# An encoder layer with two groups of attention heads: the grid heads' matrix work in equal sets with scores six steps ahead, value transposes in projection banks, the last projection ended half by half

## The chip, the core and the metric

One Trainium2 chip, of which one core is used. The core has a matrix engine (TensorE, PE in the rows; its weight loads are PEld), a vector engine (VectorE, DVE), a scalar engine (ScalarE, ACT), a fourth engine (GpSimd, POOL), and a queue engine (SyncE, SP) that issues DMAs. Each engine takes its own instructions in order; semaphores make one wait for another. Matrix products land in PSUM, of which this kernel uses eight banks of 128 partitions x 512 float32. The metric is the device time of one execution in microseconds (us); lower is better.

## What is computed

One layer on `x` of 1024 tokens x 1024 features, in float32: a normalized projection, two token mixers side by side, an output projection, and a gated MLP. Cut to the parts that the change touches:

```python
hn = rmsnorm(x, norm_mix)
qa, ka, va, qb, kb, vb = split(hn @ w_in)       # 1024 x 2304
# group A: 8 heads of 64, 2 key/value heads, |i - j| <= 128, rotary, a sink logit
o_a = window_gqa_sink(rope(qa), rope(ka), va, sink)
# group B: 8 heads of 64; tokens are a grid of 16 rows x 64 columns,
# each attends to a window of 8 x 16 grid positions, with a bias per head and offset
o_b = neighbourhood_attention(qb, kb, vb, rpb)
mix = concat(rmsnorm(o_a, norm_a), rmsnorm(o_b, norm_b))
h = x + mix @ w_out
out = rmsnorm(h + conv_gated_mlp(rmsnorm(h, norm_ffn)), norm_final)
```

In group B, for each head: scores `s = q k^T / 8 + bias` over the neighbourhood, `p = softmax(s)`, `o = p v`.

## The kernel before

**Layout and precision.** Features lie on partitions and tokens along the free dimension: eight tiles of 128 x 1024 hold the activations. A product of two float32 matrices is done as three matmuls of a faster type (fp32r) on operands split in a high and a low part, high x high, high x low and low x high. So every operand passes a split first: ScalarE copies the high part, VectorE subtracts it for the low part. A *projection block* is these three matmuls of 512 columns for one 128-row chunk of the contraction: `block()`, L177 to L179.

**Projections.** `Project(m)`, m = 0 to 17, each makes 128 of the 2304 columns of `w_in` for all tokens, in two halves of 512 tokens with 8 blocks each. m < 6 feeds group A, m >= 6 the grid heads (group B): of each three, one makes the values of a pair of heads (6, 9, 12, 15) and the next two make query and key of one head each. Head h's q and k come from m = 7 + h + h // 2, so head 6's from 16 and head 7's from 17, the last. Each projection takes a PSUM bank of the tag `pj` for each half; when a half is done, VectorE multiplies it with the tokens' inverse norm and reorders it (`evacuate()`, L251 for the grid). The projection's operands are `xg`, the split input.

Then the result is made ready for attention (`post()`):
- `split_qk()` for a grid head: for each half, ScalarE writes the scaled high part `a` (L306), VectorE the low part `b` (L307); then four DMAs of 256 KB on SP's queue stack queries and keys: q[0:64] from a (L309), q[64:128] from b (L310), b[0:64] from a (L311), a[0:64] from b (L312). Tile `a` is called ka and `b` kb. L311 overwrites rows that L310 reads.
- `split_v()` for a pair's values: TensorE transposes four chunks of 128 tokens into one bank (L334), ScalarE copies the high part (L338) and VectorE subtracts (L339), for each of the two heads; then the same for the other four chunks. The first group uses a bank of the tag `pj` and is issued at once; the second is put in the list `later` with a count of 2, so that it comes two blocks further on, in a bank of the tag `pt`, which is that of the probability transposes.

Behind the projections, `OutA(d)`, d = 0 to 7, does the half of the output projection that needs group A only, and adds `x` (L623). Its operands `mg` are the split of `mix[0:4]`, made during projection 17 by `split()` (L189 for the high, L190 for the low part, a whole tile of 128 x 1024 each).

**Attention over the grid.** For each of 8 heads and each block b of 128 tokens (8 columns of the grid):
- *score* (`q_step`): two matmuls of 256 or 384 columns (L389), against ka and then kb, into a bank `s`; VectorE adds the bias and takes the extreme in one pass (L412), ScalarE takes exp (L416); at every second block VectorE takes reciprocals (L418) and GpSimd scales the probabilities (L420);
- *transposes* (`t_step`): two or three transposes of 128 x 128 of the probabilities into a bank `pt` (L526); ScalarE copies the high part ph (L426), VectorE makes the low part pl (L427);
- *value product* (`v_step`): a matmul with ph (L537) and one with pl (L538) of 256 or 384 columns into banks `o`, two per head; at a half's end `leave()` moves it out (L552, L554) into mix[4:8].

The window attention of group A has the same three steps, with its own lines (L452 transposes, L457 and L458 value products, L474 the way out).

**Order.** TensorE's order is written by hand: the program's order of matmuls is the engine's. VectorE, ScalarE and the queues are ordered by a scheduler that has priorities (`high_priority`) and a few fixed orders (`behind`). Each tag of PSUM, `pj`, `pt`, `s` and `o`, has two banks that are taken in turn.

The hand-written order mixes attention steps with projection blocks. The attention is a list of *units* u (16 for group A; then four per grid head, with the transposes steps [0], [1, 2], [3, 4] and [5, 6, 7]). In each unit a list of *events* is made: for each transposes step "t", then "v", and scores "q" put between them at fixed places. A "v" runs the value product of the transposes step *before*. After each event, projection blocks come from a generator `filler`, as many as a running `debt` says; `RATES` gives the blocks per eight window units or per grid head. So the blocks between a transposes step and its value product are what covers the split L426 and L427:

```python
            for i, item in enumerate(mine):
                events.insert(min(EVA[i] if kind == 0 else 2 * i + 1, len(events)), ("q", item))
            wi = u // 8 if u < 16 else 2 + (u - 16) // 4
            per = RATES[wi] / (8 if u < 16 else 4) / len(events)
```

The scores taken in unit u are those up to unit u + 2. A score whose projection is not finished makes `run_q` pull blocks from the filler first. `settle()` runs once per block: it counts down `later`, and starts `post()` of a projection LAG = 3 blocks (for 17: SOON = 1) behind its end.

Some other work is put at fixed blocks of the filler: the squares of mix[0:4] (L200), their sums over features (`add_up()`, L209 transposes and L210 the reduction), `widen()` (L240) and the eight normalizations of mix[0:4] with group A's gain (`normed_a`, L816), all during projections 14 to 16; at heads 6 and 7 the squares of mix[4:7] (`square_b`, L880). `halve_w()` (L170 and the line behind it) splits the weights. At the very start, L707 and neighbours are the first three projections, run chunk by chunk as the input arrives; L146 is a set of matmuls on ones ahead of them. The MLP behind the attention has lines from L960 on.

Of the kernel before, what the change touches and what calls it, by code (L numbers as in the profile page):

```python
# [20 lines left out]
KT = D // 128  # L21
# [12 lines left out]
RATES = [41, 50, 21, 21, 21, 21, 13, 19, 20, 17]  # L34
SPARE = (3, 6)
AHEAD = 4
EVA = (1, 3, 5, 8)
# [19 lines left out]
def hybrid_layer(tc, xT, w_first, w_in, w_out, w_gate, w_up, w_down, small, sink, rpb, consts, rope, out):  # L57
    nc = tc.nc
    with ExitStack() as ctx:
# [126 lines left out]

        def split(src, name, tag):
            hi, lo = big(name + "h", tag, F32R), big(name + "l", tag, F32R)
            nc.scalar.activation(hi, src, AF.Copy)  # L189
            nc.vector.tensor_tensor(lo, src, f32(hi[:, :]), op=ALU.subtract)  # L190
            return hi, lo
# [135 lines left out]
        def split_v(t, halves, then=None):  # L327
# [13 lines left out]
            if then is None:  # L341
                group(0)
                group(1)
            else:
                with tc.high_priority(offset=500):
                    group(0, "pj")
                later.append([2, lambda: (group(1), then())])
# [215 lines left out]
        class Project:  # L563
# [10 lines left out]
            def run(self):  # L574
# [7 lines left out]
                else:  # L582

                    ps = [bank("pj", "pj") for _ in range(2)]
                    for k in range(KT):
                        for h in range(2):
                            block(ps[h], self.w[k], xg[k], h, k == 0, k == KT - 1)
                            yield
                        if k % 2:
                            mg[k // 2] = split(mix[k // 2], "mg", "xg")  # L590
                    with tc.high_priority(offset=500):
                        for h in range(2):
                            evacuate(self.t, ps[h], h, self.grid)

            def post(self):
                post(self.m, self.t)
                if self.m < 6 or self.m % 3:
                    done.add(self.m)

# [263 lines left out]
        def run_q(items):  # L863
            for u, s in items:
                while any(m not in done for m in flat[u][2]):
                    assert next(filler)
                s()
# [19 lines left out]
        for u in range(len(flat)):  # L887
            q, t, need, kind = flat[u]
            if kind == 0 and u < 14:
                mine = q_until(u + 2, 4)  # L890
            else:
                mine = q_until(min(u + 2, len(flat) - 1), 99)
            events = []
            for ts in t:
                events += [("t", ts), ("v", None)]
            for i, item in enumerate(mine):
                events.insert(min(EVA[i] if kind == 0 else 2 * i + 1, len(events)), ("q", item))
            wi = u // 8 if u < 16 else 2 + (u - 16) // 4
            per = RATES[wi] / (8 if u < 16 else 4) / len(events)
            if u in (40, 44):  # L900
                square_b(u)
            for what, e in events:
# [9 lines left out]
                fill(int(debt))  # L912
# [696 lines left out]
```

## Time and profile before

| | before |
|---|---|
| time, median of 3 runs | 1026.67 us (1026.21 to 1027.19) |
| time of the profiled execution | 1027.14 us |
| its span on the core, from the first to the last recorded instruction | 1025.3 us |
| TensorE matmuls, busy | 1011.5 us, 99% |
| TensorE weight loads (beside the matmuls) | 890.5 us, 87% |
| VectorE busy | 836.6 us, 82% |
| ScalarE busy | 562.0 us, 55% |
| GpSimd busy | 108.6 us, 11% |

How to read the profile: times are microseconds from the start of the span; an operation is written out<-in by the names of the program's tiles; "L177" is a line of the kernel. A timeline row has the start, the duration, the engine, the line, the operation with its tiles and shapes, and in brackets how long the engine had stood idle before it and which instruction ended that wait. "x3" at the end is three instructions run together in one row. "SPq" is the issue of a DMA from SP's queue. Matmuls are pipelined and their ends are modelled, so that a row's duration is longer than the time until the next one can start. A row of waits has the waiting engine and operation, what released it, the microseconds in all, how often, and the longest.

The attention over the grid runs from about 170 to 352 us, mixed with projections 6 to 17 and OutA.

### The profile page before, as it was taken

How to read it: one execution, taken by the hardware profiler on the slowest of the kernel's cores; microseconds unless marked ns; L12 is line 12 of the kernel's file. 1: busy time of each engine (PE TensorE's matmuls, PEld its weight loads, DVE VectorE, ACT ScalarE, POOL GpSimd, SP SyncE). 2: the span in 40 equal slices, each digit the busy share in tenths (PEclk: the TensorE clock that was granted, in tenths of full speed). 3: DMA queues.
4: the chain of work that ended last, by engine and by line, in shares of the span. 5: the costliest groups of instructions: out<-in, count | busy, mean ns of one | idle time of the engine just before them, and what ended most of it. 6: DMA issues, size and time to landing. Idle time of an engine off the chain costs nothing.

```text
span 1025.3 us, 14859 instructions
## 1 busy us (share of the span) xinstructions
PE 1011.5 (99%) x5094; PEld 890.5 (87%) x5094; DVE 836.6 (82%) x1566; ACT 562.0 (55%) x1077; POOL 108.6 (11%) x188
## 2 busy tenths in 40 slices
PE   9999999999999999999999999999999999999996
PEld 8888888888888888888888888888888888888886
DVE  7889887768878799999987777786787877996765
ACT  8567776657676544565545444443544645554451
POOL 0233332232342100000000000000000000000002
PEclk9999999999999999999999999999999999999999
DMA  7223022323226257213442332233322888966644
GB/s 292 77 77 95 30 73 62 93 72 84 81 62 185 76 161 267 93 61 105 156 186 100 129 117 96 100 113 113 102 108 98 285 295 297 306 228 236 224 151 165
DMA packets 68220, 144.94 MB, mean 141 GB/s; under 512 B 8240, under 2 KB 18736, under 8 KB 68144
## 3 DMA queue, kind: packets, MB, share of 16 engines
q1 hardware_dynamic: 58064, 118.82, 36.1%
q10 hardware_dynamic: 10080, 25.17, 6.3%
q8 instruction: 40, 0.66, 0.3%
q14 instruction: 36, 0.29, 0.1%
HBM read 103.58 MB, written 28.57 MB: 129 GB/s over the span
## 4 chain that ended last, share of the span: by engine, by line
PE 84%; DVE 10%; ACT 4%; issue 2%; DMA 1%; DVEq 0%; POOL 0%; ACTq 0%; POOLq 0%
PE dn L994 7%; PE dn L992 7%; PE dn L993 6%; PE pj L177 6%; PE pj L178 6%; PE pj L179 6%; PE x L992 6%; PE x L993 6%; PE x L994 6%; PE y L994 3%; PE y L993 3%; PE y L992 3%; PE s L389 3%; PE z L994 2%; PE z L992 2%
## 5 line engine op out<-in xcount | busy, mean ns | idle before, releaser
L992 PE MATMUL x<-hg,whi 128*128 128x512 f32 x352 | 133.6, 380 | 0.9 <-ACT gs L1034 0.9
L993 PE MATMUL x<-hg,whi 128*128 128x512 f32 x352 | 133.4, 379 | 0.0
L994 PE MATMUL x<-hg,wlo 128*128 128x512 f32 x352 | 133.4, 379 | 0.0
L992 PE MATMUL dn<-xd,whi 128*128 128x512 f32 (+1 forms) x330 | 120.8, 366 | 0.0
L993 PE MATMUL dn<-xd,whi 128*128 128x512 f32 (+1 forms) x330 | 120.5, 365 | 0.0
L994 PE MATMUL dn<-xd,wlo 128*128 128x512 f32 (+1 forms) x330 | 120.5, 365 | 0.0
L416 ACT ACTIVATE p<-p,nm 128x385 f32<-128x385 f32 (+3 forms) x128 | 75.1, 588 | 53.9 <-DVE nm L412 50.7
L420 POOL TENSOR_SCALAR p<-p,sm 128x384 f32<-128x384 f32 (+1 forms) x128 | 79.7, 635 | 204.6 <-DVE sm L418 177.8
L966 ACT ACTIVATE whi<-ws 128x512 fp32r<-128x512 f32 (+1 forms) x100 | 60.8, 622 | 72.0 <-DVE ws L1106 16.6
L177 PE MATMUL pj<-xgh,whi 128*128 128x512 f32 x245 | 99.7, 407 | 0.0
L178 PE MATMUL pj<-xgl,whi 128*128 128x512 f32 x245 | 92.9, 379 | 0.0
L179 PE MATMUL pj<-xgh,wlo 128*128 128x512 f32 x245 | 92.9, 379 | 0.0
L966 ACT ACTIVATE whi<-raw 128x512 fp32r<-128x512 f32 (+1 forms) x102 | 61.0, 612 | 44.1 <-PE x L993 20.3
L967 DVE TENSOR_TENSOR wlo<-ws,whi 128x512 fp32r<-128x512 f32 (+1 forms) x100 | 66.8, 682 | 19.9 <-ACT whi L966 19.6
L427 DVE TENSOR_TENSOR pl<-pt,ph 128x384 fp32r<-128x384 f32 (+2 forms) x108 | 63.5, 589 | 20.5 <-ACT ph L426 18.4
L1314 ACT ACTIVATE xd<-xd 128x512 fp32r<-128x512 f32 x77 | 47.7, 628 | 53.3 <-DMA xd<-x 52.6
L1429 POOL TENSOR_TENSOR h<-h,wide 128x256 f32<-128x256 f32 (+1 forms) x6 | 5.4, 915 | 670.9 <-ACT wide L1425 670.9
L992 PEld LDWEIGHTS x<-hg,whi 128*128 128x128 f32 x352 | 66.5, 189 | 10.9 <-ACT gs L1034 1.5
L994 PEld LDWEIGHTS x<-hg,wlo 128*128 128x128 f32 x352 | 66.5, 189 | 9.5
L993 PEld LDWEIGHTS x<-hg,whi 128*128 128x128 f32 x352 | 66.5, 189 | 9.3
L1315 DVE TENSOR_TENSOR xd<-xd 128x512 fp32r<-128x512 f32 x77 | 52.5, 690 | 27.0 <-ACT xd L1314 26.8
L992 PEld LDWEIGHTS dn<-xd,whi 128*128 128x128 f32 x330 | 62.5, 189 | 7.7
(267 smaller groups left out, 2535.4 us busy)
## 6 DMA issues: line engine op xcount, KB each, us to landing
xd<-x SPq DMA_DIRECT2D x77, 256.0 KB, 5.1
raw<-in_w_down_dram SPq DMA_DIRECT2D x72, 256.0 KB, 4.4
raw<-in_w_gate_dram SPq DMA_DIRECT2D x22, 512.0 KB, 3.4
raw<-in_w_up_dram SPq DMA_DIRECT2D x22, 512.0 KB, 3.6
x<-c ACTq DMA_DIRECT2D x22, 512.0 KB, 2.6
raw<-in_w_in_dram SPq DMA_DIRECT2D x30, 256.0 KB, 2.8
raw<-in_w_down_dram SPq DMA_DIRECT2D x36, 192.0 KB, 4.5
x<-t ACTq DMA_DIRECT2D x11, 512.0 KB, 2.6
```

The source lines that it names most:

```text
L177: nc.tensor.matmul(ps, w[0], mv(x[0][:, tsl(h)]), start=first, stop=False)
L178: nc.tensor.matmul(ps, w[0], mv(x[1][:, tsl(h)]), start=False, stop=False)
L179: nc.tensor.matmul(ps, w[1], mv(x[0][:, tsl(h)]), start=False, stop=last)
L416: nc.scalar.activation(p[:, j, 0:e], p[:, j, 0:e], AF.Exp, bias=nm, scale=-1.0, accum_out=sm[:, j:j + 1])
L420: nc.gpsimd.tensor_scalar(p[:, i, 0:m], p[:, i, 0:m], sm[:, i:i + 1], 1.0, op0=ALU.mult, op1=ALU.mult)
L427: mark["rest"] = nc.vector.tensor_tensor(pl[:, 0:n], ps[:, 0:n], f32(ph[:, 0:n]), op=ALU.subtract)
L966: nc.scalar.activation(hi, src, AF.Copy)
L967: nc.vector.tensor_tensor(lo, src, f32(hi[:, :, :]), op=ALU.subtract)
L992: nc.tensor.matmul(ps, w[0], x[0], start=first and i == 0, stop=False, skip_group_check=True)
L993: nc.tensor.matmul(ps, w[0], x[1], start=False, stop=False, skip_group_check=True)
L994: nc.tensor.matmul(ps, w[1], x[0], start=False, stop=last and i == len(ws) - 1, skip_group_check=True)
L1315: nc.vector.tensor_tensor(lo, f32(lo), f32(hi), op=ALU.subtract)
```

## The change

The same matmuls, splits and transfers are done in another order and in part in other banks; the last projection's operands are split in other pieces.

- *Equal sets.* In the grid, each transposes step now opens a set of its own: the transposes, one score, the value product of the step before. Each set gets one eighth of the head's projection blocks, spread evenly over its events. Before, a unit's blocks were spread over its events, so a unit with three transposes steps had as many blocks as one with a single step.
- *Scores six steps ahead.* One score is taken per set (three in the first), so that the score of block b + 6 goes with the transposes of chunk b. `GRID_AHEAD = 6`. The last window units take their scores in as before, without a limit of four.
- *Rates.* `RATES` changes by one block in heads 2, 3, 6 and 7. Blocks that `run_q` pulls are now taken off the debt.
- *Second half of the value transposes.* It comes 8 blocks later in place of 2, in a bank of the tag `pj`, at high priority.
- *Last projection.* For the first six chunks the halves alternate as before; then half 0 gets its last two chunks, and half 1 its last two. Each half is evacuated as soon as its last block is issued. The splits of mix[0:4] are done by halves (`split_part`: 128 x 512), eight in place of four of each kind; `split()` is gone.

```diff
@@ -31,9 +31,10 @@
 
 LAG, LATE, SOON = 3, 13, 1
 FILL0, FILL1 = 22, 14
-RATES = [41, 50, 21, 21, 21, 21, 13, 19, 20, 17]
+RATES = [41, 50, 21, 21, 22, 22, 13, 19, 19, 16]
 SPARE = (3, 6)
 AHEAD = 4
+GRID_AHEAD = 6
 EVA = (1, 3, 5, 8)
 WARM = 8
 
@@ -183,12 +184,6 @@
             for i, (w, x) in enumerate(zip(ws, xs, strict=True)):
                 block(ps, w, x, h, i == 0, i == len(ws) - 1)
                 yield
-
-        def split(src, name, tag):
-            hi, lo = big(name + "h", tag, F32R), big(name + "l", tag, F32R)
-            nc.scalar.activation(hi, src, AF.Copy)
-            nc.vector.tensor_tensor(lo, src, f32(hi[:, :]), op=ALU.subtract)
-            return hi, lo
 
         def squares(tiles, engine):
             acc = None
@@ -344,7 +339,12 @@
             else:
                 with tc.high_priority(offset=500):
                     group(0, "pj")
-                later.append([2, lambda: (group(1), then())])
+                def second():
+                    with tc.high_priority(offset=500):
+                        group(1, "pj")
+                    then()
+
+                later.append([8, second])
             return [x[:, :].rearrange("p (c w) -> p c w", w=128) for x in v]
 
         qa, ka, va, qb, kb, vb = {}, {}, {}, {}, {}, {}
@@ -582,20 +582,33 @@
                 else:
 
                     ps = [bank("pj", "pj") for _ in range(2)]
-                    for k in range(KT):
-                        for h in range(2):
-                            block(ps[h], self.w[k], xg[k], h, k == 0, k == KT - 1)
-                            yield
-                        if k % 2:
-                            mg[k // 2] = split(mix[k // 2], "mg", "xg")
-                    with tc.high_priority(offset=500):
-                        for h in range(2):
-                            evacuate(self.t, ps[h], h, self.grid)
+                    order = [(k, h) for k in range(KT - 2) for h in range(2)] + [(k, h) for h in range(2) for k in (KT - 2, KT - 1)]
+                    parts = []
+                    for k, h in order:
+                        block(ps[h], self.w[k], xg[k], h, k == 0, k == KT - 1)
+                        if k == KT - 1:
+                            with tc.high_priority(offset=500):
+                                evacuate(self.t, ps[h], h, self.grid)
+                        yield
+                        if parts:
+                            split_part(*parts.pop(0))
+                        if h and k % 2:
+                            i = k // 2
+                            mg[i] = big("mgh", "xg", F32R), big("mgl", "xg", F32R)
+                            split_part(i, 0)
+                            parts.append((i, 1))
+                    for part in parts:
+                        split_part(*part)
 
             def post(self):
                 post(self.m, self.t)
                 if self.m < 6 or self.m % 3:
                     done.add(self.m)
+
+        def split_part(i, h):
+            src, (hi, lo) = mix[i][:, tsl(h)], (t[:, tsl(h)] for t in mg[i])
+            nc.scalar.activation(hi, src, AF.Copy)
+            nc.vector.tensor_tensor(lo, src, f32(hi), op=ALU.subtract)
 
         class OutA:
             def __init__(self, d):
@@ -861,9 +874,11 @@
             return res
 
         def run_q(items):
+            nonlocal debt
             for u, s in items:
                 while any(m not in done for m in flat[u][2]):
                     assert next(filler)
+                    debt -= 1
                 s()
 
         sums = {}
@@ -886,20 +901,23 @@
         fill(FILL1 - 12)
         for u in range(len(flat)):
             q, t, need, kind = flat[u]
-            if kind == 0 and u < 14:
-                mine = q_until(u + 2, 4)
+            events = []
+            if kind == 0:
+                mine = q_until(u + 2, 4 if u < 14 else 99)
+                for ts in t:
+                    events += [("t", ts), ("v", None)]
+                for i, item in enumerate(mine):
+                    events.insert(min(EVA[i], len(events)), ("q", item))
+                rate = [RATES[u // 8] / 8 / len(events)] * len(events)
             else:
-                mine = q_until(min(u + 2, len(flat) - 1), 99)
-            events = []
-            for ts in t:
-                events += [("t", ts), ("v", None)]
-            for i, item in enumerate(mine):
-                events.insert(min(EVA[i] if kind == 0 else 2 * i + 1, len(events)), ("q", item))
-            wi = u // 8 if u < 16 else 2 + (u - 16) // 4
-            per = RATES[wi] / (8 if u < 16 else 4) / len(events)
+                rate = []
+                for ts in t:
+                    mine = q_until(len(flat) - 1, 1 if events or u > 16 else GRID_AHEAD - 3)
+                    events += [("t", ts)] + [("q", item) for item in mine] + [("v", None)]
+                    rate += [RATES[2 + (u - 16) // 4] / 8 / (2 + len(mine))] * (2 + len(mine))
             if u in (40, 44):
                 square_b(u)
-            for what, e in events:
+            for (what, e), per in zip(events, rate, strict=True):
                 if what == "t":
                     nxt = e()
                 elif what == "v":
@@ -909,8 +927,9 @@
                 else:
                     run_q([e])
                 debt += per
-                fill(int(debt))
-                debt -= int(debt)
+                due = max(0, int(debt))
+                fill(due)
+                debt -= due
             live["op"] -= 7 if u in (7, 15) else 4 if u >= 16 and u % 4 == 3 else 0
         with tc.high_priority(offset=500), behind("high"):
             nc.scalar.activation(warm, eps, AF.Sqrt)
```

## The prediction, on record before the changed kernel ran

> **What bounds the kernel now.** I read the page first: engine shares, then the windows by stage, then who waited for whom, then the timeline at each wait.
>
> ```profile
> span 1025.3 us, 14859 instructions
> PE 1011.5 (99%) x5094; PEld 890.5 (87%) x5094; DVE 836.6 (82%) x1566; ACT 562.0 (55%) x1077; POOL 108.6 (11%) x188
> 265.00:270.00 5.00, 5.00 (x35) 4.56 (x33) 4.61 (x10) 3.05 (x9) 1.47 (x2) 1.00 0.20 59
> 270.00:275.00 5.00, 3.92 (x21) 3.07 (x20) 4.87 (x12) 2.71 (x7) 1.44 (x2) 1.00 0.14 40
> 275.00:280.00 5.00, 5.00 (x34) 4.61 (x33) 4.94 (x13) 3.29 (x9) 0.07 (x1) 1.00 0.03 13
> ...
> PE o L538 <- DVE pl L427: 2.0, 5, 1.0
> PE pj L177 <- DVE t L251: 0.7, 1, 0.7
> PEld pt L526 <- POOL p L420: 0.4, 1, 0.4
> PEld pt L526 <- DVE pl L427: 0.3, 1, 0.3
> ```
>
> TensorE sets the time: 99% busy. (A window's row: length; busy time of PE, weight loads, DVE, ACT, POOL; clock; DMA.) A change of order removes no matmul, so it can only win back waits, and those that it can reach lie in the attention over the grid, from 170 to 352 us; the last four rows (waiter, releaser, us in total, times, longest) are for that stretch. VectorE is nearly full there for a while: 4.61 + 4.87 + 4.94 = 14.4 of 15 us.
>
> A matmul's end in the trace is modelled, so an idle figure hides part of a wait. I price waits by distances between starts.
>
> ```profile
> 204.53 0.43 PE L537 MATMUL o<-ph,v 128*128 128x384 f32 x1
> 205.12 0.43 PE L538 MATMUL o<-pl,v 128*128 128x384 f32 x1 [0.16 <-DVE pl L427]
> ...
> 271.66 0.38 PE L179 MATMUL pj<-xgh,wlo 128*128 128x512 f32 x1
> 272.12 0.43 PE L537 MATMUL o<-ph,v 128*128 128x384 f32 x1
> 273.55 0.43 PE L538 MATMUL o<-pl,v 128*128 128x384 f32 x1 [0.99 <-DVE pl L427]
> 273.81 0.38 PE L526 MATMUL pt<-cst,p 128*128 128x128 f32 x2
> ...
> 291.08 0.43 PE L537 MATMUL o<-ph,v 128*128 128x384 f32 x1 [0.31 <-ACT ph L426]
> 291.68 0.43 PE L538 MATMUL o<-pl,v 128*128 128x384 f32 x1 [0.16 <-DVE pl L427]
> ...
> 312.73 0.33 PE L537 MATMUL o<-ph,v 128*128 128x384 f32 x1
> 313.55 0.43 PE L538 MATMUL o<-pl,v 128*128 128x384 f32 x1 [0.49 <-DVE pl L427]
> ```
>
> A 384-column matmul follows the one before it after 0.16 us when nothing hinders it. L538 came after 0.59, 1.43, 0.60 and 0.82: late by 0.43, 1.27, 0.44 and 0.66. L537 was late by 0.24 at 272.12 (0.46 behind L179 where 0.22 is usual) and idle for 0.31 at 291.08. That makes 3.35; the waits' five plus a shorter one are six places, so two more at about 0.35 each, and each restart costs 0.1 more (273.55 to 273.81 is 0.26): 3.35 + 0.7 + 0.6 = **4.65 us** for value products waiting for a split.
>
> ```profile
> 309.45 0.33 PE L389 MATMUL s<-kb,q 128*128 128x384 f32 x1
> 309.61 0.49 PE L526 MATMUL pt<-cst,p 128*128 128x128 f32 x3
> 310.81 0.45 PE L177 MATMUL pj<-mgh,whi 128*128 128x512 f32 x1 [0.71 <-DVE t L251]
> ...
> 324.12 0.27 PE L389 MATMUL s<-ka,q 128*128 128x256 f32 x1
> 324.51 0.38 PE L389 MATMUL s<-kb,q 128*128 128x256 f32 x1
> ```
>
> The first output block waited for the last projection's evacuation: idle 0.71, with what the modelled end hides **1.0**. Head 7's first score waited for a DMA into kb: 0.39 between starts instead of 0.11, with its restart **0.4**. Transposes waiting (the two PEld rows), a short wait of project 17 for a bank and some below 0.1: **1.0**. In all 4.65 + 1.0 + 0.4 + 1.0 = about **7.1 us** that a better order could win.
>
> **The change, part by part.** I compared the order of instructions on each engine in both programs; the matmuls are the same ones.
>
> *Equal sets and scores ahead.* The value product of chunk 6 of each head used to start 1.84 us of TensorE work after the end of its transposes (a projection block of three matmuls 0.65, a value product 0.32, two transposes 0.22, a block 0.65), once 1.2. That with a wait of 0.43 to 0.66 means that the split is ready after about 2.3 to 2.5 us. In the new order the least distance in all grid heads is 2.49 and the usual one 3.4 to 5. So the waits for splits go, except where VectorE itself is behind. From 265 to 280 it worked 14.4 us while TensorE did only some 13.1 us of work (15 less waits of 1.5 at 272 and 0.3 at 282). The same VectorE work still falls on the same matmuls (the four subtractions of the value split, the eight normalizations L816), so a debt of 1.3 stays, of which the extra distance (0.65 and more) absorbs a part. I put **1.0 us** of waits there, between 0 (all absorbed) and 1.8 (as before).
>
> *What that order brings forward.* Scores six steps ahead also means that the first score of a head comes earlier behind the projection that makes its q and k. That is the part that costs.
>
> ```profile
> 292.38 0.38 PE L178 MATMUL pj<-xgl,whi 128*128 128x512 f32 x1
> 292.60 0.38 PE L179 MATMUL pj<-xgh,wlo 128*128 128x512 f32 x1
> 293.12 0.68 DVE L251 TENSOR_TENSOR t<-pj,rstd 128x512 f32<-128x512 f32 x1
> 293.84 1.34 ACT L306 ACTIVATE ka<-t,cst 128x512 fp32r<-128x512 f32 x2 [1.09 <-DVE t L251]
> 294.60 1.41 DVE L307 SCALAR_TENSOR_TENSOR kb<-t,cst,ka 128x512 fp32r<-128x512 f32 x2
> 296.04 0.47 SPq L310 DMA_DIRECT2D q<-kb  x1
> 299.34 0.46 SPq L311 DMA_DIRECT2D kb<-ka  x1
> 302.42 0.27 PE L389 MATMUL s<-ka,q 128*128 128x256 f32 x1
> ...
> 309.07 0.38 PE L179 MATMUL pj<-xgh,wlo 128*128 128x512 f32 x1
> 317.01 1.42 DVE L307 SCALAR_TENSOR_TENSOR kb<-t,cst,ka 128x512 fp32r<-128x512 f32 x2
> 318.45 0.47 SPq L310 DMA_DIRECT2D q<-kb  x1
> 321.53 0.46 SPq L311 DMA_DIRECT2D kb<-ka  x1
> ```
>
> Read the first chain: project 16's last matmul gives way at 292.81; evacuation, high part, low part, a DMA that reads kb (3.30 until the next can go), a DMA that overwrites kb. By the second chain the score's kb matmul starts 2.98 behind that last issue (321.53 to 324.51). So 3.23 + 3.30 + 2.98 = 9.5 us, and head 6's first score came 9.6 us behind: just in time, nothing to spare. In the new order three projection blocks (1.95) and a 384-column score (0.32) fewer and one transpose (0.11) more lie between, and the 0.2 wait of project 17 is out: 9.6 - 1.95 - 0.32 + 0.11 - 0.2 = 7.25 us, 7.35 to the kb matmul. Even with every engine at once at hand that is 9.5 - 7.35 = 2.1 late. It won't be: in the new order the second L306 stands on ScalarE behind an exponential and the split of head 5's first transposes, and the second L307 on VectorE behind two splits and the reduction (0.63) of a score that TensorE finishes only 2.7 us behind the projection. L310 then leaves after some 2.9 + 0.63 + 0.72 + 0.2 = 4.4 to 4.7 instead of 3.23, so the wait is 3.3 to 3.6; I take **3.4 us**, from 2.1 (no queueing) to 4.4 (VectorE another 0.8 behind). Queued behind it on TensorE is everything, since its order is fixed; VectorE and ScalarE catch up meanwhile.
>
> The Trainium skill (DMA: Bandwidth & Descriptors, "Anatomy of one DMA") gives about 2.0 us fixed plus the bytes over 436 GB/s, for DMAs issued by GpSimd; for 256 KB that would be an estimated 2.6, two of them 5.2 instead of the 6.3 measured, and the forecast 1.1 lower. The measured rows decide.
>
> Head 7: the first score was 324.12 - 309.29 = 14.8 us behind project 17, 13.1 without the waits between. Now it is 10.2 (three blocks, a score, a value product and three transposes fewer), 10.3 to kb. The chain is shorter too, because VectorE's order puts both L307 right behind the next weights and no longer behind two sums of squares and an output add: evacuated 1.4 behind the projection (one bank is free earlier now), then 2.1 of other VectorE work, 1.4 of L307, so L310 after 4.9 where it was 9.2, and kb after 4.9 + 6.3 = 11.2. I put **0.9**, from 0 (L310 after 4.0) to 1.5.
>
> *Value transposes through a projection bank.* The second group's bank is wanted by a projection block 2.0 us later at the closest place; two copies and two subtractions of about 0.4 go before, with one score's reduction between. I put **0.3**, from 0 to 0.5. What it frees, the transposes' own bank, is in the 7.1.
>
> *Last projection by halves.* Half 0 is evacuated two blocks earlier, so the 1.0 goes: the first output block comes 2.3 us behind the end of half 0, and the evacuation stands second on VectorE by then. Eight half-size splits replace four whole ones; their cover is the slack of ScalarE (55% busy), and if it is gone their cost is in the debt above. Nothing changes before 170 us but one value split's place, and nothing behind the attention.
>
> **The sum.** 7.1 goes, 1.0 + 3.4 + 0.9 + 0.3 = 5.6 comes: 1.5 us gained. The profiled execution took 1027.14 us, 0.47 above the median of 1026.67; 1027.14 - 1.5 = 1025.6, or against the median **1025.2 us**. The likeliest case's own range is 1024.0 to 1026.4.
>
> **Rivals.** *All of it is won.* The new waits stay at their lower ends (2.1 at head 6, nothing else): 7.1 - 2.1 = 5.0 gained, 1021.7. For it speaks that distances grew everywhere else; against it the chain of 9.5 us, measured. *The waits only move.* VectorE's debt stays whole (1.8), head 6 waits 4.4, head 7 1.5, the bank 0.5, sum 8.2: 1.1 lost, 1027.8. For it speaks the 14.4 of 15 us; so the change does not do what it says. *Slower: the pause slows TensorE's clock.*
>
> ```profile
> 0.99 3.78 PE L146 MATMUL warm_ps<-ones 128*128 128x128 f32 x16 [0.99 <-POOL eps L141]
> 6.59 0.61 PE L707 MATMUL o<-xgh,wlo 128*128 128x512 f32 x1
> 7.02 0.40 PE L707 MATMUL s<-xgh,wlo 128*128 128x512 f32 x1
> 7.25 0.38 PE L707 MATMUL pj<-xgl,whi 128*128 128x512 f32 x1
> ```
>
> At the start 512 columns take 0.43 us, and from 7.02 on 0.23 and less: from 0.99 to 7.02 TensorE ran at half pace, which is worth 3.0 us. If head 6's pause put it back there, that price is paid again. The longest pause in this trace without harm is 1.43 (273.55); the point from which it decides lies above. With a pause of 4.4 and this price the gain of 1.5 becomes 0.5 - 3.0 = a loss of 2.5: 1029.2. The Trainium skill (TensorE: Matmul & The Clock Gate, "The HAM clock gate") puts the fall to half rate behind one idle window of about 3.4 us that runs freely; the forecast pause is just there, so mostly no whole window would fit in. No run here has shown such a pause.
>
> **How the numbers follow.** Forecast 0.5, all won 0.2, only moved 0.2, clock 0.1. Range 1022.4 to 1028.2: it leaves out half of the first rival and the last. About 0.2% (2.05 us) is what a measurement of this kernel tells from no change. Faster (below 1024.6): the first rival and 0.15 of the forecast's lower part, 0.35. Slower (above 1028.7): the clock and 0.02 of the moved waits, 0.12. Same: 0.53.
>
> **What will show it.** Right: a wait of 3 us or more before head 6's first score matmul (L389, released by the DMA into kb), a wait below 1.5 at head 7's, no wait before the first output block, L538 waiting in the stretch of the L816 normalizations at most. Wrong: no such pause at head 6 (then the chain was shorter than I read it), value products waiting in many heads, or a granted clock below 1.00 behind the pause.

## The result: 0.24% slower

Thirteen executions of each kernel: 1029.76 us for the changed kernel (median; 1027.20 to 1032.43) against 1027.24 before (1026.21 to 1028.62). The ratio is 1.0024, with a 95% interval of 1.0014 to 1.0034: slower by 2.5 us. The changed kernel's executions lie 5.2 us apart, those of the kernel before 2.4, and the time goes with the mean clock that TensorE was granted (1 is full speed). Five of the thirteen, in order:

| time, us | 1027.20 | 1028.02 | 1029.50 | 1030.09 | 1032.19 |
|---|---|---|---|---|---|
| mean clock | 0.998 | 0.996 | 0.995 | 0.994 | 0.992 |

Over all thirteen a thousandth of the clock goes with about 0.9 us, but not exactly: the three executions at 0.996 took 1028.02 to 1029.76. The only one at 0.998 took 1027.20, what the kernel before takes.

The profiled execution took 1031.37 us, 1.6 above the median: it shows more of the loss than the usual one. Line numbers have shifted: the blocks L177 to L179 are now L178 to L180, the evacuation L251 is L246, L306/L307 are L301/L302, the DMAs L309 to L312 are L304 to L307, the value split's subtraction is L334, and the squares' sum L880 is L895. Attention lines L389 to L538 are unchanged. The kernels of the experiments have shifted lines of their own; there the tiles tell what a row is: s<-ka,q and s<-kb,q are a score's two matmuls, pt<-cst,p transposes of probabilities, pj<-xgh a projection block, pj<-mgh an output block.

First the page's span and TensorE's clock in 40 slices, of the changed kernel:

```profile
span 1029.6 us, 14879 instructions
PEclk9999999999989999999999999999999999999998
```

The one low slice inside is the twelfth, 283 to 309 us. The waits of TensorE there (165 to 360 us), in the view of waits, as microseconds in all, times, longest:

```profile
PE s L389 <- DMA ka<-kb: 2.5, 1, 2.5
PE s L389 <- DMA kb<-ka: 1.5, 2, 0.8
PE s L389 <- DVE nm L412: 0.9, 1, 0.9
PE pj L178 <- DVE v L334: 0.7, 1, 0.7
PE pj L178 <- DVE t L246: 0.2, 1, 0.2
```

No value product waits for a split in this list any more, and no output block for the last projection. In their place scores wait for DMAs. The windows of the same execution (length; busy PE, weight loads, DVE, ACT, POOL; clock; DMA share; GB/s):

```profile
270.00:275.00 5.00, 5.00 (x31) 4.58 (x30) 4.93 (x10) 1.98 (x6) 0.84 (x2) 1.00 0.03 7
275.00:280.00 5.00, 5.00 (x33) 4.51 (x31) 4.94 (x14) 3.43 (x9) 1.47 (x2) 1.00 0.13 46
295.00:300.00 5.00, 2.61 (x16) 2.00 (x14) 5.00 (x12) 4.92 (x12) 1.69 (x1) 1.00 0.82 179
300.00:305.00 5.00, 4.05 (x11) 3.24 (x12) 3.61 (x6) 1.64 (x4) 2.83 (x4) 0.57 0.14 30
305.00:310.00 5.00, 5.00 (x24) 4.50 (x23) 1.77 (x6) 2.16 (x5) 1.04 (x2) 0.75 0.00 0
```

VectorE is as full from 270 to 280 as before, but TensorE no longer waits there. It stands still in the window behind 295, and from 300 to 310 its clock is down. The timeline at that place, from project 16's last matmul on:

```profile
289.47 0.38 PE L180 MATMUL pj<-xgh,wlo 128*128 128x512 f32 x1
289.69 0.38 PE L526 MATMUL pt<-cst,p 128*128 128x128 f32 x2
...
291.07 0.69 DVE L246 TENSOR_TENSOR t<-pj,rstd 128x512 f32<-128x512 f32 x1
...
291.81 0.48 PE L178 MATMUL pj<-xgh,whi 128*128 128x512 f32 x1 [0.22 <-DVE t L246]
...
294.49 1.01 DVE L302 SCALAR_TENSOR_TENSOR kb<-t,cst,ka 128x512 fp32r<-128x512 f32 x1
...
295.52 0.47 SPq L305 DMA_DIRECT2D q<-kb  x1
...
297.24 0.38 PE L180 MATMUL pj<-xgh,wlo 128*128 128x512 f32 x1
...
298.40 0.46 SPq L306 DMA_DIRECT2D kb<-ka  x1
...
300.15 0.35 PE L389 MATMUL s<-ka,q 128*128 128x256 f32 x1 [2.54 <-DMA ka<-kb]
...
301.30 0.58 PE L389 MATMUL s<-kb,q 128*128 128x256 f32 x1 [0.80 <-DMA kb<-ka]
...
301.67 0.63 PE L178 MATMUL pj<-xgh,whi 128*128 128x512 f32 x1
...
302.10 0.63 PE L179 MATMUL pj<-xgl,whi 128*128 128x512 f32 x1
```

This is the forecast pause. The first score of head 6 starts 2.91 us behind the last matmul of the block ahead (297.24 to 300.15) instead of 0.22, and its second matmul 1.15 behind the first instead of 0.11: 2.7 + 1.0 = 3.7 us. Behind it a 512-column matmul takes 0.43 us instead of 0.22. The half pace ends here:

```profile
306.57 0.63 PE L179 MATMUL pj<-xgl,whi 128*128 128x512 f32 x1
307.00 0.63 PE L180 MATMUL pj<-xgh,wlo 128*128 128x512 f32 x1
307.43 0.37 PE L537 MATMUL o<-ph,v 128*128 128x384 f32 x1
307.64 0.33 PE L538 MATMUL o<-pl,v 128*128 128x384 f32 x1
```

Between 301.30 and 307.43 lie three projection blocks (0.65 each unhindered), a value product and a score of 384 columns, three transposes (0.33 each of these) and a score matmul (0.11): 3.05 us of work in 6.13. The slow clock cost 3.1 us in this execution.

The span is 4.3 us longer than that of the profiled execution before. Between the last value product of the window attention and the last one of the grid it is 3.5 us longer, little more than the slow clock alone. A part of the rest lies far behind the attention, where TensorE waits twice for ScalarE in the MLP instead of once. From the waits of the whole executions, the changed kernel's and that of before:

```profile
PE x L1011 <- ACT gs L1053: 1.8, 2, 0.9
PE x L992 <- ACT gs L1034: 0.9, 1, 0.9
```

This wait is there once or twice in the profiles of the experiments too (0.8 to 1.6 us in all), in both orders; it is not counted as a part of the change.

### The profile page after: what moved, and what is told of

It is laid out like the page before. It is cut to its first block, busy times and chain, and to the rows that moved or that the text cites. A ratio compares the mean times of both kernels' runs of the same rounds, so it can differ in the third digit from the quotient of the medians.

```text
span 1029.6 us, 14879 instructions
## 1 busy us (share of the span) xinstructions
PE 1012.8 (98%) x5094; PEld 893.1 (87%) x5094; DVE 834.8 (81%) x1570; ACT 563.8 (55%) x1081; POOL 107.5 (10%) x188
## 4 chain that ended last, share of the span: by engine, by line
PE 82%; DVE 11%; ACT 3%; DMA 3%; issue 2%; DVEq 0%; POOL 0%; SPq 0%; ACTq 0%
PE pj L178 7%; PE dn L1011 6%; PE dn L1012 6%; PE dn L1013 6%; PE pj L180 6%; PE pj L179 6%; PE x L1011 6%; PE x L1012 6%; PE x L1013 6%; PE y L1011 3%; PE y L1013 3%; PE y L1012 3%; PE s L389 3%; PE z L1013 2%; PE z L1011 2%
## 5 line engine op out<-in xcount | busy, mean ns | idle before, releaser
L178 PE MATMUL pj<-xgh,whi 128*128 128x512 f32 x245 | 100.5, 410 | 1.0 <-DVE v L334 0.7
L179 PE MATMUL pj<-xgl,whi 128*128 128x512 f32 x245 | 93.6, 382 | 0.0
L180 PE MATMUL pj<-xgh,wlo 128*128 128x512 f32 x245 | 93.6, 382 | 0.0
L986 DVE TENSOR_TENSOR wlo<-raw,whi 128x512 fp32r<-128x512 f32 (+1 forms) x102 | 66.2, 668 | 3.7 <-ACT whi L985 3.7
```

Of the source, the lines that this page charges most:

```text
L178: nc.tensor.matmul(ps, w[0], mv(x[0][:, tsl(h)]), start=first, stop=False)
L179: nc.tensor.matmul(ps, w[0], mv(x[1][:, tsl(h)]), start=False, stop=False)
L180: nc.tensor.matmul(ps, w[1], mv(x[0][:, tsl(h)]), start=False, stop=last)
L986: nc.vector.tensor_tensor(lo, src, f32(hi[:, :, :]), op=ALU.subtract)
```

## The experiments

All times are medians; each is compared with the kernel before in runs on the same chip, and the ratio has a 95% interval. The kernel before showed mean clocks of 0.996 to 0.998 in these runs, 0.996 in 5 of 53 executions.

**Is it the pause that slows the clock?** Theory A says so; B says the clock falls for another reason. First the pause was filled with work whose result is not used.

```diff
-        def scores(q, k, b):
+        def scores(q, k, b, extra=0):
...
             ps = bank("s", "s")
             qs = q[:, b * 128:(b + 1) * 128]
+            for _ in range(extra):
+                nc.tensor.matmul(ps, xg[7][0][:, 0:128], mv(xg[7][0][:, 0:HALF]), start=True, stop=True)
...
-                    ps, n = scores(qb[h], kb[h], b)
+                    ps, n = scores(qb[h], kb[h], b, 12 if (h, b) == (6, 0) else 0)
```

> The changed kernel, with 12 more matmuls of 512 columns put before head 6's first score; they write the score's own bank, which that score then starts anew, so the output stays. They are 12 x 0.216 = 2.6 us of work in a pause of 2.7. Theory A (the pause before head 6's first score sets off the slower clock that the profile shows from 301 to 307 us, worth 3.1 us): the score comes as late as before, but no matmul behind it shows the half pace, and the time falls by about 3 us from the changed kernel's 1029.8, to 1026 to 1027.5, with a mean clock of 0.998. Rival B (the slower clock has another cause, the denser order or the heads behind): the clock stays at 0.994 to 0.996 and the time at 1029.8.

Measured: 1028.52 us (1026.52 to 1029.16, 11 executions), ratio 1.0007 (0.9998 to 1.0016). The half pace behind head 6 is gone from the profile, which took 1027.27 at a mean clock of 0.998. Five of the eleven executions had 0.998 and took 1026.5 to 1027.9; three had 0.996 and took 1029.0 to 1029.2. The view of waits of this kernel says why the gain is smaller than A expected:

```profile
PE s L391 <- DMA kb<-ka: 1.6, 2, 0.8
PE s L391 <- DMA ka<-kb: 1.4, 1, 1.4
```

The 1.4 is at head 7. Without half pace TensorE arrives there earlier, while VectorE and the DMAs come no sooner. So head 7's pause grew from 1.9 to 2.65 us in all (1.60 ahead of the ka matmul, 1.05 ahead of kb), and in the executions at 0.996 it may have cost clock in its turn; in the profiled one it did not. Both pauses were filled next (7 matmuls before head 7's first score too).

> The changed kernel with both pauses filled: 12 matmuls of 512 columns before head 6's first score and 7 (1.5 us) before head 7's, in the bank that the score then starts anew. With head 6's pause filled alone, head 7's grew to 1.6 + 1.05 us, and some executions still showed a mean clock of 0.996. Theory A (pauses alone slow the clock): no execution below 0.997, the median at that of the quick executions with one filling, 1027.2, with less spread. Rival B (some other half of the clock loss is not from pauses): still 1028.5 with clocks down to 0.996.

Measured: 1027.96 us (1027.30 to 1028.93), ratio 1.0007 (0.9998 to 1.0015), and no execution below 0.997; the profile shows no half pace. The clock did what A says. The median is 0.8 above A's number and no better than with one filling by the ratio; A had taken the five quick executions for the whole. Against 1029.76 the clock's share of the loss is 1.8 us by the medians, 1.7 by the ratios (1.0024 less 1.0007). The two intervals just meet (1.0014 and 1.0015), so this size is uncertain by more than 1 us. The waits that are left cost within the interval what the waits before had cost.

Then the other way round: pauses made in the kernel before, by copying rows into kb again (the same data), which only lengthens the chain of DMAs.

```diff
                 mark["stacked"] = nc.sync.dma_start(f32(b[0:64, :]), f32(a[64:128, :]))
+                for _ in range(again):
+                    nc.sync.dma_start(f32(b[0:64, :]), f32(a[64:128, :]))
...
-                    qb[h], kb[h] = split_qk(t)
+                    qb[h], kb[h] = split_qk(t, 1 if h == 6 else 0)
```

> The kernel before, with one DMA more in head 6's chain: the copy of a[64:128] into b[0:64] is made twice, with the same data. The chain that was just in time is then some 3.0 us late. Theory A: a pause of about 3 us before head 6's first score (its kb matmul), and in most executions half pace behind it for some us: 1026.7 + 3 + 1 to 3 = 1031 to 1033 and a mean clock of 0.995 to 0.997. Rival B (the clock does not hang on the pause): + 3.0 alone, 1029.7 to 1030, clock 0.998.

> The kernel before with a small DMA more in head 6's chain (128 of the 1024 columns of b[0:64] copied again, the same data). Expected pause before the kb matmul: 2.5 less some 0.8 = 1.7 us. Theory A (a pause slows the clock only from some length between 1.4 and 2.5 us on): clock 0.997 to 0.998 as before, no half pace behind the pause, and 1027 to 1028, since the pause gives back other waits, as the pause of 2.5 did. If the point lies below 1.7: clock down to 0.996 in part of the executions, 1028.5.

> The kernel before with the copy of a[64:128] into b[0:64] made three times: the pause before head 6's kb matmul should be 2.5 + 2.8 = 5.3 us. Theory A (the longer the pause, the surer and longer the half pace behind it): every execution slowed, the mean clock at 0.992 to 0.994, half pace for 3.4 to 7 us, and 1029.0 + 2.8 + 1 to 3 = 1033 to 1035. Rival B: 1031.8, with the clock no lower than with the pause of 2.5 (0.996).

| kernel before with | pause | median, us | ratio (interval) | mean clocks |
|---|---|---|---|---|
| 128 columns copied again | 1.43 | 1027.37 | 0.9997 (0.9988 to 1.0006) | 0.997 to 0.998 |
| all copied again | 2.54 | 1029.04 | 1.0015 (1.0006 to 1.0024) | 0.995 to 0.997 |
| all copied twice more | 5.37 | 1033.42 | 1.0053 (1.0039 to 1.0067) | 0.994 to 0.995 |

The pause is the distance between head 6's two first score matmuls beyond 0.11. The timeline with 2.54, TensorE alone:

```profile
301.93 0.27 PE L391 MATMUL s<-ka,q 128*128 128x256 f32 x1
304.58 0.38 PE L391 MATMUL s<-kb,q 128*128 128x256 f32 x1 [2.38 <-DMA kb<-ka]
304.79 0.38 PE L177 MATMUL pj<-xgh,whi 128*128 128x512 f32 x1
305.01 0.38 PE L178 MATMUL pj<-xgl,whi 128*128 128x512 f32 x1
...
306.22 0.63 PE L177 MATMUL pj<-xgh,whi 128*128 128x512 f32 x1
306.65 0.63 PE L178 MATMUL pj<-xgl,whi 128*128 128x512 f32 x1
...
309.79 0.43 PE L177 MATMUL pj<-xgh,whi 128*128 128x512 f32 x1
310.06 0.38 PE L178 MATMUL pj<-xgl,whi 128*128 128x512 f32 x1
```

TensorE works at full pace again for 1.4 us behind the pause, and only then falls to half for some 3.4 us (about 306.0 to 309.4). Of the eleven executions six had a mean clock of 0.996 or less; the other five, at 0.997, can't be told from the kernel before. With 5.37 TensorE is at half pace from the pause's end on, for 4.5 us, and the time of 1033.42 is A's (1033 to 1035), not B's (1031.8):

```profile
307.55 0.58 PE L391 MATMUL s<-kb,q 128*128 128x256 f32 x1 [5.21 <-DMA kb<-ka]
307.92 0.63 PE L177 MATMUL pj<-xgh,whi 128*128 128x512 f32 x1
...
311.33 0.63 PE L179 MATMUL pj<-xgh,wlo 128*128 128x512 f32 x1
311.76 0.62 PE L528 MATMUL pt<-cst,p 128*128 128x128 f32 x3
312.14 0.46 PE L177 MATMUL pj<-xgh,whi 128*128 128x512 f32 x1
```

And with 1.43, at no place. So A stands in the old order too: no other part of the change is needed to slow the clock. The point from which a pause counts lies between 1.43 and 2.54 us in these runs. One expectation missed: the pause of 2.54 was to cost 4 us or more and cost 1.6, less than its own length. VectorE catches up in it: the first output block, which waited 1.0 us for the evacuation in the kernel before, does not wait in this profile, nor in that with 1.43, where the pause and the waits won nearly balance. (The short pause came out at 1.43, not 1.7.)

**Is all the loss at heads 6 and 7?** The pause was taken away by letting sets of head 5 take no score, so that the scores are four or five steps ahead from there on (lead four, lead five).

```diff
-                    mine = q_until(len(flat) - 1, 1 if events or u > 16 else GRID_AHEAD - 3)
+                    mine = q_until(len(flat) - 1, 0 if (u, t.index(ts)) in [(37, 1), (38, 0)] else 1 if events or u > 16 else GRID_AHEAD - 3)
```

> The changed kernel, but two sets of head 5 (chunks 2 and 3) take no score, so that from head 6 on the scores run four steps ahead instead of six, and head 6's first score comes two sets, some 3.9 us of TensorE work, later. Theory A (all that the change loses is the pauses at heads 6 and 7 and what the first does to the clock): the waits of 3.7 and 1.9 and the clock's 3.1 go, so 1029.8 - 8.7 = about 1021, 0.5% below the kernel before. Rival C (the waits move on: with a lead of four the splits or the score's banks wait instead, or the equal sets lose elsewhere): 1025 or more, with new waits in heads 6 and 7.

> The changed kernel, with one set of head 5 (chunk 2) that takes no score: the lead is five from head 6 on, and head 6's first score comes some 1.95 us of work later. Theory A: the pause shrinks from 3.7 to 1.8 us in all; a pause as short as the 1.4 that did no harm in the kernel before should not slow the clock, so 1029.8 - 1.9 - 1.0 (head 7) - 3.1 = about 1023.8, clock 0.998. Rival B: the clock stays low, 1026.9.

Measured: lead four 1024.08 us, ratio 0.9969 (0.9957 to 0.9980); lead five (only (37, 1) in the list) 1024.30, ratio 0.9970 (0.9959 to 0.9982). Lead five came out half a microsecond from A's number, with 0.36 + 1.05 left ahead of head 6's first score, no half pace and next to nothing at head 7. Lead four has neither pause, but is 3 us above A: C is right in part. A had taken the clock's 3.1 of the profiled execution off the median; with the 1.8 of the medians its sum is 1022.4. The longest wait is a new one, where transposes reach probabilities that GpSimd has not scaled yet:

```profile
PE pt L526 <- POOL p L420: 1.8, 1, 1.8
```

With it the sum is 1024.2, and 1024.08 was measured.

**What are the other two parts worth?** Each was undone in the version with lead five.

```diff
-                def second():
-                    with tc.high_priority(offset=500):
-                        group(1, "pj")
-                    then()
-
-                later.append([8, second])
+                later.append([2, lambda: (group(1), then())])
```

> The changed kernel with one set of head 5 that takes no score (1024.3 us), and with the second group of the value transposes put back: two blocks later, in a bank of the transposes, without priority. Theory A (the projection bank is taken too long: the changed kernel's projection block waits 0.8 us for the second group's last subtraction): that wait goes and nothing replaces it, 1023.5. Rival D (what the projection bank costs, the probability transposes' bank would cost too): 1024.3 or above, with waits of probability transposes for the subtraction of the value split.

Measured: 1024.15 us, ratio 0.9967 (0.9955 to 0.9980) against 0.9970 with lead five alone: D's number, no difference between the banks that these intervals show. The wait that goes is this one, in the changed kernel, where the projection block comes 0.99 us behind the last value product (0.16 is usual):

```profile
194.49 0.33 PE L538 MATMUL o<-pl,v 128*128 128x384 f32 x1
...
194.91 0.42 DVE L334 TENSOR_TENSOR v<-vt,v 128x256 fp32r<-128x256 f32 x1
...
195.48 0.45 PE L178 MATMUL pj<-xgh,whi 128*128 128x512 f32 x1 [0.66 <-DVE v L334]
```

What comes in its place is, by the waits of that experiment, in another head (at 279.00 and 281.31). The releaser is the split of the probabilities, not the subtraction of the value split that D had named:

```profile
PE pt L521 <- DVE pl L422: 1.3, 2, 0.8
```

The last projection was put back to its old form, `split()` and both evacuations at its end included:

```diff
-                    order = [(k, h) for k in range(KT - 2) for h in range(2)] + [(k, h) for h in range(2) for k in (KT - 2, KT - 1)]
...
+                    for k in range(KT):
+                        for h in range(2):
+                            block(ps[h], self.w[k], xg[k], h, k == 0, k == KT - 1)
+                            yield
+                        if k % 2:
+                            mg[k // 2] = split(mix[k // 2], "mg", "xg")
```

> The changed kernel with one set of head 5 that takes no score (1024.3 us), and with the last projection as before: halves alternating to the end, both evacuated at the end, splits of whole tiles. Theory A (ending it half by half wins the 1.0 us that the first output block waited): 1025.3, with that wait back at the first output block. Rival E (in the new order the evacuation is in time either way): 1024.3, no such wait.

Measured: 1023.24 us, ratio 0.9958 (0.9946 to 0.9971). A falls, and E is not quite it either: the old form is no worse, and if anything better (the intervals of 0.9970 and 0.9958 overlap). Its timeline at the first output block, TensorE and then VectorE:

```profile
308.01 0.49 PE L532 MATMUL pt<-cst,p 128*128 128x128 f32 x3
308.33 0.45 PE L178 MATMUL pj<-mgh,whi 128*128 128x512 f32 x1
```

```profile
307.49 1.41 DVE L252 TENSOR_TENSOR t<-pj,rstd 128x512 f32<-128x512 f32 x2
```

Both halves are evacuated in one go (1.41 us), the first is done at about 308.2, and the output block starts at 308.33 with no wait. So the halves are not needed for it. That the equal sets did it is not shown: this version still pauses for some 1.5 us at head 6, and the kernel before, with neither sets nor halves, loses this wait too when it pauses there (for 1.43 or 2.54 us).

**A better version.** Lead five, the split of q and k of heads 6 and 7 with priority on ScalarE and VectorE, and the rates moved.

```diff
-RATES = [41, 50, 21, 21, 22, 22, 13, 19, 19, 16]
+RATES = [41, 50, 21, 21, 22, 22, 14, 20, 18, 15]
...
+            with tc.high_priority(offset=500 if soon else 0):
+                for h in range(2):
+                    nc.scalar.activation(a[:, tsl(h)], t[:, tsl(h)], AF.Copy, scale=by)
+                    nc.vector.scalar_tensor_tensor(b[:, tsl(h)], t[:, tsl(h)], by, f32(a[:, tsl(h)]), op0=ALU.mult, op1=ALU.subtract)
...
-                    qb[h], kb[h] = split_qk(t)
+                    qb[h], kb[h] = split_qk(t, h > 5)
```

> The changed kernel with one set of head 5 that takes no score (1024.3 us), with priority for the split of q and k of heads 6 and 7 on ScalarE and VectorE, and with one projection block more in each of heads 4 and 5 and one less in each of heads 6 and 7. Head 6's first score then comes two blocks (1.3 us) later behind its projection and its chain should be about 1 us shorter. Theory A: the 1.4 us that it still waits go, and head 7's 0.2: 1022.7. Rival C: with fewer blocks in heads 6 and 7 value products or transposes wait there instead, 1024 or more.

> The version with five scores ahead from head 6 on, priority for the split of q and k, and the moved rates (1022.7 us), and with the last projection as before, its halves alternating to the end. Theory A (ending it half by half costs 1.0 us here, as the comparison 1024.3 to 1023.2 said): 1021.7, and no wait at the first output block. Rival E (that difference belonged to the 1.4 us pause at head 6, which this version no longer has): 1022.7.

> The same as the version before it in this call, and with the second group of the value transposes two blocks later in a bank of the probability transposes, as in the kernel before. Theory D (either bank costs the same): as the version before it, within 0.3 us, with the projection block's wait of 0.8 replaced by waits of probability transposes.

Measured: 1022.74 us, ratio 0.9952 (0.9938 to 0.9965); with the last projection as before as well 1022.11, 0.9946 (0.9933 to 0.9958); with the value transposes as before too 1021.53, 0.9942 (0.9930 to 0.9955). None of the three has a wait at head 6's or 7's first score. But with that pause gone the first output block's wait came back, which the second expectation had ruled out: 1.1 us with the halves (the first two rows, VectorE's and TensorE's), 1.0 without them (the third row), 0.6 in the last version.

```profile
305.33 0.68 DVE L246 TENSOR_TENSOR t<-pj,rstd 128x512 f32<-128x512 f32 x1
306.16 0.45 PE L178 MATMUL pj<-mgh,whi 128*128 128x512 f32 x1 [0.90 <-DVE sm L419]
306.29 0.46 PE L178 MATMUL pj<-mgh,whi 128*128 128x512 f32 x1 [0.80 <-ACT ph L433]
```

In each of them, as in the kernel before, the block starts 0.15 us behind the end of half 0's evacuation (here 305.33 + 0.68); the releasers named are later, small instructions. With the halves, half 0's last block had given way at 302.70. Its evacuation came 2.6 us later, because VectorE's order has a split, a score's reduction and a subtraction for the weights ahead of it; VectorE even stood idle for 1.05 us before that split. Why the wait is back is open: priority and rates moved in these versions too, so the missing pause is not the only difference, and lead four, with no pause there either, does not have this wait.

The last version came out 0.6 us below the one before it, where D allowed 0.3; the steps among these three lie inside their intervals. It is 0.6% faster than the kernel before. What it keeps of the change is the equal sets and scores that run ahead.

## Why the prediction was wrong

The forecast was a gain of 1.5 us; the result is a loss of 2.5, outside the range. The third rival, the pause that slows TensorE's clock, gave 1029.2 with a chance of 0.1, and 1029.76 came. That it is so near is in part luck: the rival has 6.6 us of waits and 3.0 of clock, where 7.1 and, by the medians, 1.8 were found.

By its steps, in the profiled execution:

| step | forecast, us | found, us |
|---|---|---|
| waits that the change removes | 7.1 | 7.1: none of them is left in the view of waits |
| VectorE's debt, 265 to 280 us | 1.0 (0 to 1.8) | 0.2, one value product at 281.95 |
| head 6's first score | 3.4 (2.1 to 4.4) | 3.7 |
| head 7's first score | 0.9 (0 to 1.5) | 1.9 |
| value transposes' bank | 0.3 (0 to 0.5) | 0.8 |
| project 17 waiting for project 16's evacuation | nothing | 0.5 |
| half pace behind head 6 | a rival, 3.0 | 3.1 (1.8 by the medians) |

*The waits that go* were read rightly, and so was the cover that takes the place of those for splits. For the 1.0 of the first output block the reason given, the earlier evacuation of half 0, is not borne out: the wait is gone without the halves in one version and there with them in another.

*Head 6* was right in size, with errors that nearly cancel. Project 16's evacuation began 1.4 us behind its last matmul (289.69 to 291.07), not 0.3, behind the reduction and the split that TensorE's new order had called for; so L305 left 5.8 us behind instead of 4.4 to 4.7. The DMAs were quicker than forecast, 2.9 + 2.9 (295.52 to 298.40 to 301.30) where 3.3 + 3.0 was read. The Trainium skill (DMA: Bandwidth & Descriptors, "Anatomy of one DMA") gave an estimated 2.6 for each: the trace is nearer to it than the kernel before was, and still above. The same late evacuation held up project 17 by 0.5, so that TensorE came to the score that much later, too.

*Head 7* was outside its bounds. Project 17's last matmul gave way at 313.86, and the chain went on like this (SyncE's queue, then TensorE, in the changed kernel):

```profile
319.10 0.47 SPq L305 DMA_DIRECT2D q<-kb  x1
...
322.04 0.46 SPq L306 DMA_DIRECT2D kb<-ka  x1
```

```profile
325.10 0.35 PE L389 MATMUL s<-ka,q 128*128 128x256 f32 x1 [0.87 <-DVE nm L412]
326.12 0.38 PE L389 MATMUL s<-kb,q 128*128 128x256 f32 x1 [0.67 <-DMA kb<-ka]
```

L305 left 5.2 us behind the projection (forecast 4.9) and L306 2.9 later. From there to the kb matmul it took 4.1 us where 3.0 had been read: 12.3 in all instead of 11.2, against the distance of 10.3 that was rightly forecast. So the term that was too small is the last DMA. The DMA engines were busier than in the kernel before (a share of 0.93 from 321 to 323 us, 0.53 before); that this is why is not shown. The wait of the ka matmul for a reduction (L412) lies inside this one: without it the kb matmul would still have started at 326.12.

So the waits nearly balance: with 0.2 + 3.7 + 1.9 + 0.8 + 0.5 = 7.1 of the 7.1 coming back, the gain of 1.5 was already gone. That agrees with the filled pauses, whose ratio of 1.0007 does not differ from 1. Of the 4.0 us between forecast and result this is 1.5 and the clock 1.8; the remaining 0.7 lies inside the interval of the result (a loss of 1.4 to 3.5 us).

*The clock* is the step that failed: the sum puts it at nothing. The prediction had the mechanism and the price (3.0; 3.1 in the profiled execution), and set its point of decision too high. It rested on the longest pause without harm in the trace of before, 1.43 between two starts (1.27 beyond the usual distance), and took the forecast 3.4 to be short of the point. The Trainium skill (TensorE: Matmul & The Clock Gate, "The HAM clock gate") puts the fall behind one idle window of about 3.4 us that runs freely, and the prediction concluded that a pause of 3.4 would mostly not fill one. The runs do not bear out that a whole window must be idle: 2.54 us of pause were enough, with a half pace that began 1.4 us later and lasted about 3.4. A window that runs freely and counts as idle when a large part of it is would fit this and the differences from one execution to the next; no run here shows the windows themselves. With the point known, this rival and the forecast were one case: a pause of 3.4 us at head 6 was the forecast, and its consequence should have been in the sum.

## What to carry to other kernels

When a wait is moved into one place, its price is not its length alone: on a TensorE that is 99% busy, several waits of 0.4 us cost what they last (the clock around those of the kernel before was 1.00), one of 2.5 us or more also costs what the slow clock takes behind it, and differently in each execution. A schedule that runs ahead must be checked at the places where its input is produced just in time: here the first score behind a projection, whose chain of evacuation, split and two DMAs got longer (9.5 us before, 11.6 after) while the distance shrank. Five steps ahead instead of six at that place turned a loss of 0.24% into a gain of 0.3%.

## What was not expected of the hardware

A pause of TensorE of 2.54 us let it run on at full pace for 1.4 us and slowed it afterwards, so the slow stretch need not touch the wait that caused it. Pauses of 1.43 left the clock alone in all 11 executions (0.997 to 0.998, within what the kernel before shows). The spread of the executions is a sign only where it is wide: 5.2 us at pauses of 2.7 + 1.0, but 2.9 at 2.54, no more than the 2.4 to 2.9 of the kernel before.
